# W2 of three feed-forward groups in four as seven products with the tokens down the partitions, summed in DRAM

## Chip, cores and metric

The kernel runs on one core of a Trainium2 chip. The metric is the time of one launch in microseconds of device time; the median of several runs stands for a kernel. The engines are TensorE (PE in the profile, with PEld for its weight loads), VectorE (DVE), ScalarE (ACT), GpSimd (POOL) and SyncE (SP), which here only issues DMAs.

## The reference, cut to what matters

Two layers, each with three token mixers on one input projection and then a feed-forward part; SEQ is 512, D_MODEL 1024, D_FF 4096, all in float32:

```
u = rms_norm(x)
[A | B | C | gates] = u @ w_in
x = x + (sigmoid gates * (branch A, B, C, projected)) @ w_out
x = x + relu(rms_norm(x) @ W1)^2 @ W2
```

The change is in the last line. W1 is 1024 by 4096, W2 4096 by 1024.

## The kernel before

**Products.** Activations lie transposed: features down the partitions, the 512 tokens along the columns. A float32 product goes in three passes over two parts of each operand, called hi and lo (type float32r): hi by hi, hi by lo, lo by hi. Weights come from DRAM in quarters of [128, 1024] floats (512 KB). SP loads a quarter into `stage`, ACT casts it to `w_hi`, DVE subtracts to give `w_lo` (`cut_to`, in the tags `hi` and `lo` of the pool `p_w`, six buffers each).

**The feed-forward part** (`mlp`). It starts with eight units `wo` (the end of the attention half), the sum of squares `ms`, and the row factors `rb`. Then come four groups. A group makes 1024 of the 4096 hidden features by W1, as four pairs of units. A pair is done as seven products of a Winograd form instead of eight (`pair`, `cut_pair`): each product has 12 matmuls of 256 columns, so a pair has 84, in PSUM tiles that the trace calls `x` (x17, x26, x45). ACT squares the relu of the outputs `c`, and ACT and DVE split them into `mh` and `ml`. The group's eight units of W2 follow, each 8 k-tiles times 3 passes = 24 matmuls of 512 columns (PSUM tile `w2`, in the trace `w`); weights are the stationary operand, `mh` and `ml` move. The first group's unit outputs are copied to `mo`, those of the next two are added to `mo` by DVE, after the third `mo` is scaled by the token factor `rs` and added to `h`, and the fourth group's are scaled into `y` and added to `h`; `ready` hands each finished row block to the next layer, whose first projection is `rv`.

**Order.** `mlp_order` weaves the next group's first two pairs of W1 into the W2 of the group before, after units 3 and 6 (`WOVEN`). All instructions are first noted, then `Plan.order` simulates a run of the engines with a price for each instruction (`price`, and `LATENCY` and `HOPS` between engines), and each engine takes the first of its ready instructions by key. So the order of every engine's stream follows from prices, from buffer counts (`BUFS_W`, `BUFS_STAGE`), and from how far ahead weights are called for (`prefetch`, `AHEAD_LOAD`, `AHEAD_SPLIT`). At run time each engine executes its stream strictly in that order. Before the change POOL issues no DMA and does nothing in the feed-forward part.

In the trace every matmul has line L411, every transpose L413, and all other engine work L417, since one helper issues them; names of tiles tell groups apart.

Of the kernel before, what the change touches and what calls it, by code (L numbers as in the profile page):

```python
# [17 lines left out]
L = 2  # L18
# [10 lines left out]
# positions of the small per-layer vectors in the row that every partition receives  # L29
# [20 lines left out]


def mlp_order():
    """W1 goes by pairs of units, W2 by units, in four groups of eight; a group's W1 starts within the W2 before it."""
    pairs = lambda g, k: [("w1", g, 2 * i) for i in k if g < 4]
    seq = pairs(0, range(4))
    for g in range(4):
        n = 0
# [9 lines left out]
def weight_plan():  # L67
    """Quarters of [128, 1024] in the order in which the core uses them: (key, matrix, rows, columns)."""
# [40 lines left out]
    for what, g, i in mlp_order():  # L109
# [3 lines left out]
        else:  # L113
            a_unit(("w2", g, i), "w_mlp_out", cols(i * 128, 128), r0=g * 1024)
    return plan
# [5 lines left out]
# units whose weights are used two by two, in seven products instead of eight (Winograd's form of Strassen's)  # L121
PAIRED = {WIDX["w1", f] for f in range(0, 32, 2)} | {WIDX["gate", n, i] for n in GATE_PAIRS for i in range(GATE_PAIRS[n], 8, 2)}

BUFS_STAGE = 2
BUFS_W = 6
BUFS_WH = 2
BUFS_MID = 3
AHEAD_LOAD = 6
AHEAD_SPLIT = 2
# [27 lines left out]

class Ref:
    """A view of such a tile."""
# [82 lines left out]
class Op:  # L242
    __slots__ = ("engine", "name", "args", "kwargs", "key", "cost", "deps", "tiles", "new", "left", "outs", "end",
                 "ready")
# [1302 lines left out]
```

## Time and profile before

| | |
|---|---|
| median of 3 runs | 1793.13 us (1792.23 to 1793.45) |
| span of the profiled execution | 1791.8 us |
| instructions | 26264 |
| granted TensorE clock | 1.00 in every slice |
| PE, DVE, ACT, POOL busy, shares of the span | 99%, 77%, 55%, 17% |

The launch has six stretches that can be told apart by the matmuls: an attention half and a feed-forward part per layer, with the eight `wo` units between them. The table of stretches further down gives each engine's busy time in one. Busy time of one instruction is longer than its share of a stream where instructions overlap in the pipeline, so the cost of one more instruction is read from the distance between the starts of neighbours (its pitch), not from its duration.

### The profile page before, as it was taken

The numbers are of one execution on the slowest core, as the hardware profiler recorded it, in microseconds if no ns is written. First come the engines' busy times: TensorE is split into PE (matmuls) and PEld (weight loads), VectorE is DVE, ScalarE is ACT, GpSimd is POOL, SyncE is SP. The second block draws the span as 40 slices with busy tenths as digits, with TensorE's granted clock in tenths as the row PEclk, the third lists the DMA queues.
The fourth block names the chain that finished last, engine by engine and source line by source line (L and its number), as shares of the span: only waits on it lengthen the run. The fifth ranks groups of instructions, "written<-read, shape, count | busy, mean of one in ns | idle before, by whom it ended". The sixth has DMA issues, their size and how long they took to land.

```text
span 1791.8 us, 26264 instructions
## 1 busy us (share of the span) xinstructions
PE 1767.7 (99%) x10216; PEld 1544.8 (86%) x10216; DVE 1376.4 (77%) x2084; ACT 983.2 (55%) x1568; POOL 297.1 (17%) x294
## 2 busy tenths in 40 slices
PE   8999999999999999999999999999999999999999
PEld 6887888889989989999888778888888899989897
DVE  7866797899979766678656677968999797566783
ACT  5545666784446655445444455768844466444450
POOL 3334472002210000000013335700111100000000
PEclk9999999999999999999999999999999999999999
DMA  6311212112352323333432121121133423234331
GB/s 203 105 61 49 93 49 79 59 37 95 107 170 101 118 94 118 123 115 116 152 106 71 48 80 62 59 63 56 39 104 130 159 83 134 95 102 128 121 113 56
DMA packets 53691, 172.50 MB, mean 96 GB/s; under 512 B 6336, under 2 KB 6848, under 8 KB 53568
## 3 DMA queue, kind: packets, MB, share of 16 engines
q1 hardware_dynamic: 53568, 170.84, 29.4%
q8 instruction: 80, 1.31, 0.3%
q14 instruction: 43, 0.35, 0.1%
HBM read 162.43 MB, written 8.39 MB: 95 GB/s over the span
## 4 chain that ended last, share of the span: by engine, by line
PE 82%; DVE 8%; issue 3%; POOL 3%; ACT 2%; DMA 1%; SPq 0%; DVEq 0%; ACTq 0%; POOLq 0%
PE x L411 21%; PE w L411 20%; PE gate L411 6%; PE proj L411 5%; PE wo L411 5%; PE c L411 4%; PE wtr L413 2%; PE rv L411 2%; DVE w_lo L417 2%; PE rg L411 2%; PE rq L411 2%; PE dsc L411 2%; PE gav L411 2%; PE gsc L411 2%; DVE c L417 1%
## 5 line engine op out<-in xcount | busy, mean ns | idle before, releaser
L417 ACT CAST w_hi<-stage 128x1024 fp32r<-128x1024 f32 (+1 forms) x283 | 276.6, 982 | 319.7 <-PE w L411 120.7
L417 DVE TENSOR_TENSOR w_lo<-stage,w_hi 128x1024 fp32r<-128x1024 f32 (+1 forms) x283 | 336.9, 1192 | 78.7 <-ACT w_hi L417 75.8
L411 PE MATMUL x<-u,w_hi 128*128 128x256 f32 x1472 | 273.5, 284 | 5.3 <-DVE c L417 5.3
L411 PEld LDWEIGHTS x<-u,w_hi 128*128 128x128 f32 x1472 | 232.3, 192 | 10.9 <-DVE c L417 8.2
L411 PE MATMUL x<-u,w_lo 128*128 128x256 f32 x736 | 208.0, 283 | 0.0
L411 PE MATMUL w<-ml,w_hi 128*128 128x512 f32 (+1 forms) x520 | 200.3, 386 | 0.0
L411 PE MATMUL w<-mh,w_lo 128*128 128x512 f32 (+1 forms) x520 | 200.1, 386 | 0.0
L411 PE MATMUL w<-mh,w_hi 128*128 128x512 f32 (+1 forms) x520 | 200.1, 387 | 0.0
L411 PEld LDWEIGHTS x<-u,w_lo 128*128 128x128 f32 x736 | 141.1, 192 | 0.0
L417 ACT ACTIVATE c<-c 128x512 f32<-128x512 f32 x156 | 98.4, 631 | 32.9 <-DVE c L417 30.2
L411 PEld LDWEIGHTS w<-mh,w_lo 128*128 128x128 f32 x520 | 97.8, 188 | 19.5
L411 PEld LDWEIGHTS w<-ml,w_hi 128*128 128x128 f32 x520 | 97.8, 188 | 18.7
L411 PEld LDWEIGHTS w<-mh,w_hi 128*128 128x128 f32 x520 | 97.8, 188 | 18.5
L411 PE MATMUL gate<-u,w_hi 128*128 128x512 f32 x320 | 107.3, 399 | 0.0
L411 PE MATMUL x<-t23h,w_lo 128*128 128x256 f32 x368 | 104.2, 283 | 0.0
L411 PE MATMUL x<-t23l,w_hi 128*128 128x256 f32 x368 | 104.0, 283 | 0.0
L411 PE MATMUL x<-t23h,w_hi 128*128 128x256 f32 x368 | 103.9, 283 | 0.0
L417 ACT CAST w_hi<-sa 128x1024 fp32r<-128x1024 f32 x46 | 48.5, 1053 | 77.0 <-DVE sa L417 55.9
L411 PE MATMUL c<-w_hi,u 128*128 128x512 f32 x256 | 86.1, 394 | 0.0
L417 POOL TENSOR_TENSOR gth<-gth,c 128x512 f32<-128x512 f32 x28 | 45.9, 1647 | 179.0 <-DVE c L417 179.0
L417 DVE TENSOR_TENSOR c<-x,pu 128x512 f32<-128x512 f32 x92 | 63.1, 686 | 12.0 <-PE x L411 11.3
L411 PEld LDWEIGHTS x<-t23l,w_hi 128*128 128x128 f32 x368 | 70.6, 192 | 0.0
(278 smaller groups left out, 4554.5 us busy)
## 6 DMA issues: line engine op xcount, KB each, us to landing
stage<-in_w SPq DMA_DIRECT2D x283, 512.0 KB, 3.6
h<-in_x SPq DMA_DIRECT2D x16, 256.0 KB, 5.3
mid<-h SPq DMA_DIRECT2D x16, 256.0 KB, 2.0
h<-mid SPq DMA_DIRECT2D x16, 256.0 KB, 4.8
keep<-h SPq DMA_DIRECT2D x8, 256.0 KB, 4.1
h<-keep SPq DMA_DIRECT2D x8, 256.0 KB, 3.9
out<-h SPq DMA_DIRECT2D x7, 256.0 KB, 2.0
t_ret<-in_t_ret SPq DMA_DIRECT2D x4, 256.0 KB, 4.9
```

Of the source, the lines that this page charges most:

```text
L411: self.nc.tensor.matmul(k.pop("out"), **k)
L413: self.nc.tensor.transpose(k["out"], k["in_"], k["identity"])
L417: getattr(getattr(self.nc, o.engine), o.name)(**k)
```

## The change

Groups 0, 1 and 2 of each layer (`WIDE_GROUPS`) do W2 in another form; group 3 keeps the eight plain units.

In a wide group the outputs have tokens down the partitions: the activations are the stationary operand (128 by 128) and W2 moves, 512 columns at a time. With W2 of the group as 2 by 2 blocks and the activations as 2 by 2 blocks, seven products are made (`WIDE_PRODUCTS`, left operands `WIDE`), each in two halves k and for two token tiles s: 24 matmuls of 512 columns per product. W1's outputs `c` are kept unsplit, and `rights` makes the right operands `xh`, `xl` from them.

The operands of the products come in three ways. A11, A12 and A22 (`cut_dma`): a DMA of POOL writes the quarter, cast, to `w_hi`; ACT writes its negative to `w_lo`; a second DMA of POOL adds the quarter onto `w_lo`. S1: a load by SP into a buffer `sa` and a DMA of POOL that adds the second quarter. S2, S4 and S3: DVE adds staged quarters; all four S are split by ACT and DVE as before.

Each product's two PSUM banks are copied by ACT to `wp` and go to `sums` in DRAM: in group 0 by plain DMAs of SP, in groups 1 and 2 by accumulating DMAs of POOL. In group 3, `gather` reads the 14 sums back, combines them with DVE, transposes the result on TensorE (PSUM tile `turn`), scales it and adds it to `h`. Its two halves stand at units 0 and 3 of that group.

Besides, `WOVEN` is (2, 4) in wide groups, `BUFS_W` falls from 6 to 5, the tag `sa` has three buffers, the prefetch goes by steps instead of quarters, the planner's price of a float32r matmul rises from 2.5 to 13.7 ns plus columns, and POOL's DMAs get prices. These alter the order of the attention half too. The diff also drops comments and docstrings; those lines are left out below.

```
-WOVEN = (3, 6)
...
+GATHERED = (0, 3)
...
+WIDE_GROUPS = (0, 1, 2)
...
+WOVEN = {True: (2, 4), False: (3, 6)}
...
-        for i in range(8):
-            while n < len(WOVEN) and WOVEN[n] == i:
+        n, wide = 0, g in WIDE_GROUPS
+        for i in range(7 if wide else 8):
+            while n < 2 and WOVEN[wide][n] == i:
...
+WIDE = ("A11", "A12", "A22", "S1", "S2", "S4", "S3")
+WIDE_PRODUCTS = (1, 2, 4, 5, 6, 3, 7)
...
-BUFS_W = 6
+BUFS_W = 5
...
-AHEAD_LOAD = 6
-AHEAD_SPLIT = 2
+AHEAD = 2
...
         if k["rhs"].tile.dtype == F32R:
-            return 2.5 + n / 2.4 * (1 if n >= 256 else 4)
+            return 13.7 + n / 2.4 * (1 if n >= 256 else 4)
...
+        o.late = self.LATENCY.get(engine, 0.0)
+        if engine == "gpsimd" and name == "dma_start":
+            o.cost, o.late = (880.0, 5600.0) if "accum_op" in kwargs else (600.0, 3800.0)
...
-        self.p_s = pool("s", 1)
+        self.p_s = pool("s", {"sa": 3, "sb": 1})
...
+    def cut_dma(self, q):
+        nc = self.nc
+        hi, lo = self.parts(self.p_w, 1024)
+        nc.gpsimd.dma_start(out=hi, in_=self.a["w"][q])
+        nc.scalar.activation(out=lo, in_=hi, func=AF.Copy, scale=-1.0)
+        nc.gpsimd.dma_start(out=lo, in_=self.a["w"][q], accum_op=ALU.add)
+        return hi, lo
...
+    def cut_wide(self, q, op, k):
+        nc = self.nc
+        at = lambda x: q + (int(x[1]) - 1) * 4 + (int(x[2]) - 1) * 2 + k
+        w = self.wide
+        def add(t, x):
+            nc.vector.tensor_tensor(out=t, in0=t, in1=self.load(at(x)), op=ALU.add)
+        if op == "A11":
+            w[k] = self.load(at("A21"), self.p_s, "sa")
+            nc.gpsimd.dma_start(out=w[k], in_=self.a["w"][at("A22")], accum_op=ALU.add)
+        if op[0] == "A":
+            return self.cut_dma(at(op))
+        if op == "S3":
+            w[k] = self.load(at("A21"))
+        if op != "S1":
+            add(w[k], {"S2": "A11", "S3": "A11", "S4": "A12"}[op])
+        return self.part(self.p_w, 1024, w[k])
+
+    def weights(self, l, key, k=0):
+        i = l * NS + STEP_AT[key] + k
+        self.prefetch(i + 1 + AHEAD)
+        return self.w[i]
...
+                    if g in WIDE_GROUPS:
+                        m.append(c)
+                        continue
...
+            if g in WIDE_GROUPS:
+                if i == 0:
+                    rights = self.rights(m)
+                    nxt = next(rights)
+                now, nxt = nxt, next(rights, None)
+                self.wide_product(l, g, i, now)
+                continue
+            if i == 0:
+                gather = self.gather(h, mid, load, r2)
+            if i in GATHERED:
+                next(gather)
...
-            if g == 0:
-                total[i] = self.g("mo")
-                nc.scalar.copy(out=total[i], in_=p)
-            elif g < 3:
-                nc.vector.tensor_tensor(out=total[i], in0=total[i], in1=p, op=ALU.add)
-                if g == 2:
-                    nc.vector.tensor_tensor(out=total[i], in0=total[i], in1=r2, op=ALU.mult)
-                    nc.vector.tensor_tensor(out=h[i], in0=h[i], in1=total[i], op=ALU.add)
...
+    def rights(self, m):
...
+        sub = lambda out, x, y: nc.vector.tensor_tensor(out=out, in0=x, in1=y, op=ALU.subtract)
+        t1 = []
+        for n in WIDE_PRODUCTS:
+            if n == 4:
+                for j in range(4):
+                    b1, b2 = m[j], m[4 + j]
+                    if j % 2 == 0:
+                        t1.append(self.g("t1"))
+                    sub(b1[:, rt], b2[:, rt], b1[:, rt])
+                    nc.vector.tensor_tensor(out=b1[:, lt], in0=b1[:, rt], in1=b1[:, lt], op=ALU.add)
+                    sub(b2[:, lt], b2[:, lt], b1[:, lt])
+                    sub(t1[-1][:, j % 2 * 256:j % 2 * 256 + 256], b2[:, rt], b1[:, lt])
+            out = []
+            for i in range(2):
+                hi, lo = self.g("xh", F32R), self.g("xl", F32R)
...
+                        self.split(x, hi[:, c], lo[:, c])
...
+    def wide_product(self, l, g, o, x):
...
+        ps = [self.psum("mm", f"wide{n}") for _ in range(2)]
+        for k in range(2):
+            hi, lo = self.weights(l, ("w2", g, o), k)
+            xh, xl = x[k]
+            for s in range(2):
+                for j in range(2):
+                    t = slice(j * 256 + s * 128, j * 256 + s * 128 + 128)
+                    c = slice(j * 512, j * 512 + 512)
+                    self.passes(ps[s], [(xh[:, t], hi[:, c]), (xh[:, t], lo[:, c]), (xl[:, t], hi[:, c])],
+                                k == 0 and j == 0, k == 1 and j == 1)
+        for s, p in enumerate(ps):
+            y = self.g("wp")
+            nc.scalar.copy(out=y, in_=p)
+            if g == WIDE_GROUPS[0]:
+                nc.sync.dma_start(out=self.sums[n, s], in_=y)
             else:
+                nc.gpsimd.dma_start(out=self.sums[n, s], in_=y, accum_op=ALU.add)
+
+    def gather(self, h, mid, load, r2):
+        def back(n, s):
+            x = self.g("wp")
+            nc.sync.dma_start(out=x, in_=self.sums[n, s])
+            return x
...
+        for s in range(2):
+            p1, p2, p6, p5, p3 = (back(n, s) for n in (1, 2, 6, 5, 3))
+            tt(p2, p1, p2)
+            tt(p6, p6, p1, ALU.subtract)
+            tt(p5, p5, p6)
+            tt(p3, p3, p5, ALU.subtract)
...
+        for half in range(2):
+            if half:
+                for s in range(2):
+                    p7, p4 = back(7, s), back(4, s)
+                    p6, p5 = u2[s]
+                    tt(p5, p5, p7, ALU.subtract)
+                    tt(p6, p6, p7, ALU.subtract)
+                    tt(p6, p6, p4)
...
+            for i in range(4):
+                k = half * 4 + i
+                h[k] = load(mid, k)
+                p = self.psum("tr", "turn")
+                for t in range(4):
+                    self.transpose(p[:, t * 128:(t + 1) * 128], c[half][t][:, i * 128:(i + 1) * 128])
                 y = self.g("y")
                 nc.vector.tensor_tensor(out=y, in0=p, in1=r2, op=ALU.mult)
...
+                nc.vector.tensor_tensor(out=h[k], in0=h[k], in1=y, op=ALU.add)
+            yield
```

Three places in the order of the engines. The first is POOL at the end of the first layer's attention half, where `gth` is a sum of gated branches and `vmu` belongs to the next layer's projection `rv`. Before:

```order
L417 TENSOR_TENSOR gth_3656<-gth_3656,c1_5396 128x512
L417 TENSOR_TENSOR gth_3882<-gth_3882,c0_5507 128x512
L417 TENSOR_TENSOR gth_4001<-gth_4001,c1_5568 128x512
L417 TENSOR_SCALAR vmu_9338<-vsum_9330 128x4
L417 TENSOR_TENSOR rs_9347<-ms_9341,mhalf_109 128x4
```

After, from the same sum on:

```order
L466 TENSOR_TENSOR gth_4017<-gth_4017,c1_5577 128x512
L466 DMA sa_6043<-in_w 128x1024
L466 DMA sa_6178<-in_w 128x1024
L466 DMA w_hi_6355<-in_w 128x1024
L466 DMA w_hi_6395<-in_w 128x1024
L466 DMA w_lo_6417<-in_w 128x1024
L466 DMA w_hi_6451<-in_w 128x1024
L466 DMA w_lo_6463<-in_w 128x1024
L466 DMA w_hi_6500<-in_w 128x1024
L466 DMA w_lo_6524<-in_w 128x1024
L466 DMA w_lo_6573<-in_w 128x1024
L466 DMA w_hi_6657<-in_w 128x1024
```

The feed-forward part now puts operand and sum DMAs into POOL's stream, one behind the other, where there was nothing between the two layers.

The second place is PE in the first group of layer 0. Before, a unit of W2 has the weight `w_hi` or `w_lo` stationary (named behind the comma) and `mh` or `ml` moving:

```order
L411 MATMUL w2_6498<-mh_6523,w_hi_6366 128x512
L411 MATMUL w2_6498<-ml_6537,w_hi_6366 128x512
L411 MATMUL w2_6498<-mh_6523,w_lo_6382 128x512
L411 MATMUL w2_6553<-mh_6169,w_hi_6386 128x512
L411 MATMUL w2_6553<-ml_6192,w_hi_6386 128x512
L411 MATMUL w2_6553<-mh_6169,w_lo_6405 128x512
```

After, around the start of product 4, whose operand A22 is `w_hi_6657` and `w_lo_6722`:

```order
L460 MATMUL x45_6752<-t4h_6066,w_hi_6489 128x256
L460 MATMUL x45_6752<-t4l_6075,w_hi_6489 128x256
L460 MATMUL x45_6752<-t4h_6066,w_lo_6511 128x256
L460 MATMUL wide4_6810<-w_lo_6722,xh_6482 128x512
L460 MATMUL wide4_6810<-w_hi_6657,xl_6502 128x512
L460 MATMUL wide4_6810<-w_hi_6657,xh_6482 128x512
L460 MATMUL wide4_6810<-w_lo_6722,xh_6482 128x512
L460 MATMUL wide4_6810<-w_hi_6657,xl_6502 128x512
L460 MATMUL wide4_6812<-w_lo_6722,xh_6482 128x512
```

The weight parts have become the moving operand, the activation parts `xh` and `xl` the stationary one, and the part that two DMAs of POOL and one copy of ACT write is read right behind the pairs of W1.

The third place is PE where W2 of the last group of layer 0 starts. Before:

```order
L411 MATMUL x26_8819<-u07_6000,w_lo_8711 128x256
L411 MATMUL w2_8930<-mh_8391,w_hi_8733 128x512
L411 MATMUL w2_8930<-ml_8404,w_hi_8733 128x512
L411 MATMUL w2_8930<-mh_8391,w_lo_8753 128x512
L411 MATMUL w2_8930<-mh_8407,w_hi_8733 128x512
```

After, `wp` being the combined sums that were read back:

```order
L460 MATMUL w2_9279<-mh_8679,w_lo_9216 128x512
L462 MATMUL turn_9338<-ident_235,wp_8937 128x128
L462 MATMUL turn_9338<-ident_235,wp_8989 128x128
L462 MATMUL turn_9338<-ident_235,wp_9070 128x128
L462 MATMUL turn_9338<-ident_235,wp_9080 128x128
L460 MATMUL w2_9279<-mh_8894,w_hi_9199 128x512
L460 MATMUL w2_9279<-ml_8905,w_hi_9199 128x512
L460 MATMUL w2_9279<-mh_8894,w_lo_9216 128x512
```

Transposes of the gathered sums, four to a tile, stand between the matmuls of the last group's units.

## Rows read from the trace of the kernel before

**Rows 1.** Page, section 1: busy time, share of the span, instructions.

```profile
span 1791.8 us, 26264 instructions
PE 1767.7 (99%) x10216; PEld 1544.8 (86%) x10216; DVE 1376.4 (77%) x2084; ACT 983.2 (55%) x1568; POOL 297.1 (17%) x294
```

**Rows 2.** Busy time by stretch: attention and feed-forward of layer 0, then of layer 1.

```profile
core 0: us, PE busy (x) PEld busy (x) DVE busy (x) ACT busy (x) POOL busy (x), PEclk, DMA share, GB/s
0.00:517.60 517.60, 504.32 (x2781) 430.24 (x2782) 425.68 (x678) 309.99 (x536) 153.95 (x156) 1.00 0.28 91
...
561.20:898.30 337.10, 337.10 (x2125) 306.73 (x2125) 242.41 (x335) 171.93 (x237) 0.00 (x0) 1.00 0.37 118
898.30:1406.00 507.70, 500.77 (x2777) 427.38 (x2776) 406.07 (x640) 294.67 (x509) 137.93 (x136) 1.00 0.25 78
...
1450.00:1791.80 341.80, 337.96 (x2151) 308.24 (x2149) 228.25 (x319) 157.09 (x216) 0.00 (x0) 1.00 0.32 105
```

**Rows 3.** Chain of waits through layer 0 feed-forward: start, us, what, matmuls.

```profile
by line: PE w L411 49.9%; PE x L411 46.1%; PE wo L411 1.8%; PE rv L411 1.7%; PE ms L411 0.4%; PE rb L413 0.1%
...
569.99 0.44 PE rb L413 x4
...
630.41 15.21 PE w L411 x67
645.62 8.63 PE x L411 x72
...
856.08 42.19 PE w L411 x186
898.26 6.12 PE rv L411 x27
```

**Rows 4.** Timeline of PE: start, us, instruction.

```profile
390.77 0.82 PE L413 MATMUL wtr<-ident,gE 128*128 128x128 f32 x6
391.34 0.48 PE L411 MATMUL gate<-u,w_hi 128*128 128x512 f32 x1
```

**Rows 5.** Timeline of DVE where its instructions stand back to back.

```profile
685.50 0.68 DVE L417 TENSOR_TENSOR sb<-stage,sa 128x512 f32<-128x512 f32 x1
686.10 0.41 DVE L417 TENSOR_TENSOR c<-x,c 128x256 f32<-128x256 f32 x1
686.44 0.68 DVE L417 TENSOR_TENSOR w_lo<-stage,w_hi 128x512 fp32r<-128x512 f32 x1
687.04 1.22 DVE L417 TENSOR_TENSOR w_lo<-sa,w_hi 128x1024 fp32r<-128x1024 f32 x1
688.19 0.69 DVE L417 TENSOR_TENSOR c<-x,pu 128x512 f32<-128x512 f32 x1
```

**Rows 6.** Groups of instructions by shape, layer 0 feed-forward: busy, mean ns | idle before.

```profile
L417 ACT CAST w_hi<-stage 128x1024 fp32r<-128x1024 f32 x52 | 54.7, 1051 | 96.2 <-PE w L411 61.3 <-PE x L411 20.4 <-DMA stage<-in_w 11.8
L417 DVE TENSOR_TENSOR w_lo<-sb,w_hi 128x1024 fp32r<-128x1024 f32 x15 | 18.3, 1219 | 5.2 <-ACT w_hi L417 5.2
L417 DVE TENSOR_TENSOR mo<-mo,w 128x512 f32<-128x512 f32 x16 | 11.0, 687 | 27.8 <-PE w L411 27.8
L417 ACT COPY mo<-w 128x512 f32<-128x512 f32 x8 | 4.6, 579 | 0.0
```

**Rows 7.** DMA in a quiet part of the feed-forward part, 600 to 850 us.

```profile
DMA packets 8369, 28.49 MB, mean 114 GB/s; under 512 B 928, under 2 KB 928, under 8 KB 8352
...
stage<-in_w SPq DMA_DIRECT2D x49, 512.0 KB, 3.6
h<-mid SPq DMA_DIRECT2D x8, 256.0 KB, 4.8
```

**Rows 8.** DMA where it is fullest, 5 to 12 us.

```profile
DMA packets 1150, 2.62 MB, mean 375 GB/s; under 512 B 125, under 2 KB 125, under 8 KB 1150
...
stage<-in_w SPq DMA_DIRECT2D x1, 512.0 KB, 6.8
```

**Rows 9.** Tile mTl, DVE beside POOL: ns min/median/max.

```profile
L417 DVE SCALAR_TENSOR_TENSOR mTl<-gth,mTh x16: 677/1235/1790, 471.8 to 1411.0; 128x512 fp32r<-128x512 f32 x16
```

**Rows 10.** Page, section 5: POOL's sums of gated branches: busy, mean ns.

```profile
L417 POOL TENSOR_TENSOR gth<-gth,c 128x512 f32<-128x512 f32 x28 | 45.9, 1647 | 179.0 <-DVE c L417 179.0
```

More of the change, by code (lines that the diff above doesn't have):

```diff
@@ L112, in weight_plan @@
                 a_unit(("w1", f), "w_mlp_in", cols(f * 128, 128))
-        else:
+        elif g not in WIDE_GROUPS:
             a_unit(("w2", g, i), "w_mlp_out", cols(i * 128, 128), r0=g * 1024)
+        elif i == 0:
+            for c in range(2):
+                for j in range(2):
+                    for k in range(2):
+                        r = g * 1024 + j * 512 + k * 256
+                        plan.append((("w2", g, c + 1, j + 1, k), "w_mlp_out", np.arange(r, r + 256), cols(c * 512, 512)))
     return plan
@@ L122, with steps @@
 PAIRED = {WIDX["w1", f] for f in range(0, 32, 2)} | {WIDX["gate", n, i] for n in GATE_PAIRS for i in range(GATE_PAIRS[n], 8, 2)}
+WIDE = ("A11", "A12", "A22", "S1", "S2", "S4", "S3")
+WIDE_PRODUCTS = (1, 2, 4, 5, 6, 3, 7)
+def steps():
+    out, at = [], {}
+    q = 0
+    while PLAN[q][0][0] != "w1":
+        at[PLAN[q][0]] = len(out)
+        out.append(("pair" if q in PAIRED else "one", q))
+        q += 2 if q in PAIRED else 1
+    for what, g, i in mlp_order():
+        at[(what, g * 8 + i) if what == "w1" else (what, g, i)] = len(out)
+        if what == "w1":
+            out.append(("pair", WIDX["w1", g * 8 + i]))
+        elif g in WIDE_GROUPS:
+            out += [("wide", WIDX["w2", g, 1, 1, 0], WIDE[i], k) for k in range(2)]
+        else:
+            out.append(("one", WIDX["w2", g, i]))
+    return out, at
+STEPS, STEP_AT = steps()
+NS = len(STEPS)
 BUFS_STAGE = 2
-BUFS_W = 6
+BUFS_W = 5
 BUFS_WH = 2
 BUFS_MID = 3
-AHEAD_LOAD = 6
-AHEAD_SPLIT = 2
+AHEAD = 2
 BUFS_G = 51
@@ L155, in tile, with __init__ @@
         return Tile(self, shape, dtype, tag or name, name).ref()
+class Pools:
+    def __init__(self, each):
+        self.each = each
+    def tile(self, shape, dtype, tag=None, name=None):
+        return self.each[tag].tile(shape, dtype, tag=tag, name=name)
 class Ref:
@@ L242 @@
 class Op:
-    __slots__ = ("engine", "name", "args", "kwargs", "key", "cost", "deps", "tiles", "new", "left", "outs", "end",
-                 "ready")
+    __slots__ = ("engine", "name", "args", "kwargs", "key", "cost", "late", "deps", "tiles", "new", "left", "outs",
+                 "end", "ready")
 class Plan:
@@ L397, in order @@
                 result.append(pick)
-                heapq.heappush(events, (now + o.cost + self.LATENCY.get(e, 0.0), 0, pick))
+                heapq.heappush(events, (now + o.cost + o.late, 0, pick))
                 heapq.heappush(events, (busy[e], 2, pick))
@@ L458, in __init__ @@
         nc.sync.dma_start(out=self.gains, in_=a["gains"])
-        self.loaded = self.cut = 0
-        self.stage, self.w = {}, {}
+        self.cut = 0
+        self.w, self.wide = {}, {}
     def tables(self):
@@ new lines, in mlp @@
+            nc.vector.tensor_tensor(out=y, in0=p, in1=r2, op=ALU.mult)
+            nc.vector.tensor_tensor(out=h[i], in0=h[i], in1=y, op=ALU.add)
+            ready(i, h[i])
+    def rights(self, m):
+        nc = self.nc
+        lt, rt = slice(0, 256), slice(256, 512)
+        sub = lambda out, x, y: nc.vector.tensor_tensor(out=out, in0=x, in1=y, op=ALU.subtract)
[13 more added lines that the diff above has]
+                hi, lo = self.g("xh", F32R), self.g("xl", F32R)
+                if n == 5:
+                    self.split(t1[i], hi, lo)
+                else:
+                    for j in range(2):
+                        k = 2 * i + j
+                        x = m[k if n in (1, 6, 7) else 4 + k][:, lt if n in (1, 2, 4, 6) else rt]
+                        c = slice(j * 256, j * 256 + 256)
+                        self.split(x, hi[:, c], lo[:, c])
+                out.append((hi, lo))
+            yield out
@@ L1435, in trunk @@
             tiles.append(k.ref())
+    core.sums = {}
+    for n in WIDE_PRODUCTS:
+        for s in range(2):
+            k = Tile(None, [128, 512], F32, None, "sums")
+            k.real = p_dram.tile([128, 512], F32, name=f"sums{n}{s}")
+            core.sums[n, s] = k.ref()
     def load(src, i):
```

97 lines of the change are left out of this document (40 added, 57 removed).

## The prediction

> **What bounds the kernel now.** First the page: TensorE (PE) is busy in 99% of the span, DVE in 77%, ACT in 55%, POOL in 17% [rows 1]. That is an average, so the table of stretches comes next. In a layer's feed-forward part PE is busy in all of the 337.1 us of layer 0, DVE in 242.4, POOL not at all, and DMA moves 118 GB/s; only in the attention halves is PE idle, 13.3 and 6.9 us [rows 2]. The chain of waits through layer 0's feed-forward part says the same in another way: it never leaves PE, half of it in W2 (`w`) and nearly half in W1 (`x`), and PE goes from the last `w` at 856.08 + 42.19 = 898.27 us straight into the next layer's `rv` [rows 3]. So here the end is set by the sum of matmul pitches, and a matmul less is worth its pitch as long as nothing else becomes late. Pitches: 512 columns 15.21 / 67 = 0.227 us, 256 columns 8.63 / 72 = 0.120 [rows 3].
>
> As a test of these prices: a layer has 32 units of 24 matmuls and 16 pairs of 84, 768 x 0.227 + 1344 x 0.120 = 335.6 of the 337.1 us.
>
> **Matmuls removed and added.** A wide group has 7 x 24 = 168 matmuls of 512 columns instead of 8 x 24 = 192. Over six wide groups that is 144 less: -144 x 0.227 = -32.7 us. A matmul with the weights moving is taken at the same price, since shape and passes are the same. Added are 64 transposes of 128 by 128. Six of them stood in (391.34 - 390.77) = 0.57 us, 0.095 each [rows 4]; the four of `rb` took 0.44, 0.11 each [rows 3]. So 6.1 to 7.0 us; I take 6.5. Net on PE -26.2 us, all on the path that sets the end. One wide group with its four pairs is now 336 x 0.120 + 168 x 0.227 = 78.5 us of PE, before 83.9.
>
> **DVE.** Its pitch, from starts of neighbours back to back, is 0.60 us for 512 elements, 0.34 for 256, 1.15 for 1024 [rows 5]. A pair costs five of 512 and three of 1024 for its weights, two of 512 and three of 256 for its outputs: 8.7 us, 34.7 for four. Before, a group added eight splits of `c`, eight `w_lo` and eight `mo`: 53.5 of 83.9 us, 64%. A wide group adds 8 `w_lo` and 6 sums of 1024, 24 splits and 16 subtractions of 256, and 2 splits of 512: 16.1 + 13.6 + 1.2 = 30.9, together 65.6 of 78.5 us, 84%. It is still under PE, so I count it at nothing; the cover is 12.9 us in a group. ACT has more cover: its idle time before the casts alone is 96 us in a layer [rows 6].
>
> **Does POOL take that cover?** POOL issues some 23 DMAs in a wide group, where it did nothing. The one place where the trace has POOL and DVE at work together is the end of the attention half: `mTl` takes 0.68 us alone but 1.24 in the median [rows 9], beside POOL's adds of 1.65 us [rows 10]. If each DMA issue held a DVE instruction up by the same 0.56 us, a group would lose 23 x 0.56 = 12.9 us of DVE, just the cover. Below that it costs nothing. The bounds for the time are 0 and about +18 (rival 2); I take 0.
> The Trainium skill, "SBUF — State Buffer", section "Who interferes with whom", says that a DVE instruction with two inputs in SBUF contends with a GpSimd instruction that reads SBUF, not with one that only writes it. The row of `mTl` agrees for adds, which read; issuing a DMA would only write descriptors, and by that rule the 12.9 us would be nothing. No row of before shows it.
>
> **The operand chain, the added wait.** For A11, A12 and A22 the path is: a slot of `p_w` comes free when its last matmul has run, POOL's DMA writes `w_hi`, ACT writes `w_lo`, POOL's second DMA adds onto it, PE reads it. Before it was shorter: the stage was loaded well ahead, and only ACT's cast waited for the slot (61.3 us of its idle time are for a `w` matmul [rows 6]). ACT's copy is 1.05 us [rows 6]. A 512 KB DMA takes 3.6 us to land when DMA is quiet [rows 7] and 6.8 when it is full [rows 8]. So the chain is 3.6 + 1.05 + 3.6 = 8.3 us at least. At most it is 6.8 + 1.05 + 6.8 and, if adding means that the target is read too, 0.524 MB / 375 GB/s = 1.4 more, 16.0 us. What does it have? In the order of PE, between the last reader of the slot of `w_hi_6657` and the first reader of `w_lo_6722` there are 19 matmuls of 512 and 84 of 256: 14.4 us. Counted so, the A operands of all wide groups have 12.9 to 14.6 us, apart from the first one of a group. So they are between 6 early and 3.1 us late. Operands come late together, in two clusters per group (A11 with A12, and A22), twelve over six groups: 0 to +37 us. POOL's queue carries the wait: behind a `w_lo` that waits for ACT stand the next `w_hi` and, in groups 1 and 2, the sums.
> Which end? Data of a wide group: 8 loads for pairs, 24 for W2's operands, 14 sums of 0.26 MB, 20.4 MB in 78.5 us, 260 GB/s. That lies 0.56 of the way from 114 [rows 7] to 375 [rows 8], so a DMA is put at 5.4 us and the chain at 11.9, a microsecond before it is due. I take three of the twelve clusters late by 1 us: +3.
> The Trainium skill, "Collectives: The Full Stack", section "The bandwidth ceiling: the fold count and why AG ≠ RS ≠ AR", says that an add made by the DMA needs two source reads. By it 7.9 MB more would be moved in groups 1 and 2, 361 GB/s, close to the fullest stretch [rows 8], the chain would be near its upper end, and the time that of rival 1; no run of before shows an adding DMA.
>
> **Gather and boundary.** The last sum that its first half needs is product 3 of group 2. From there ACT's copy 0.6 [rows 6], the adding DMA 3.6 to 6.8, the read back at 4.8 [rows 7] and eight DVE adds of 0.60, all pessimistically in a row, are 14 to 17 us. By the order PE has 22.7 us of other matmuls before the first transpose. The transposes stand in PE's stream, so if they are late PE stops. After the last pair of W1, counted in the order at these pitches, DVE now has 46 us of work in layer 0 beside 47 us of PE; before the change 30 beside 45. Bounds 0 and +5 for each layer; I take +2 in all.
>
> **Attention half.** The planner's new matmul price and five buffers for six reorder it. Rows of its effect don't exist; the bounds are the PE idle time that there is, 20 us over both layers, as a gain or as a loss [rows 2]. I take 0, with 7 either way as usual size, for the work itself is the same.
>
> **Sum.** 1791.8 - 26.2 + 3 + 2 = 1770.6 us of span; the median of before stands 1.3 us above the profiled span, so 1771.9, said as 1772.
>
> **Rivals.**
> 1. The operand chain is late, and the kernel ends no faster or slower. For it: 16.0 us at the upper end, POOL's single queue, 360 GB/s if adds read twice. Against: DMA was quiet before, and 11.9 us by the interpolated landing. At 12 clusters it eats the gain when it is late by (26.2 - 2) / 12 = 2.0 us, and is slower by over 0.2% from 2.3 us on. Late by 1 to 3.1 us it gives 1781 to 1806; at 2.3, 1797.
> 2. DVE becomes the bound in the wide groups, by POOL's interference on top of 84%. For it: [rows 9]. Then the waits of DVE for ACT, which cost nothing today, count as well: with 2 to 3 us in each of six groups 12 to 18 us, and the late boundary 5 more. It gives 1780 to 1795.
> 3. The attention half moves by its new order more than the feed-forward part: 1752 to 1792.
> That the columns don't go is excluded, since the order has 144 matmuls of 512 less.
>
> **How the numbers follow.** Measurement tells 0.2% (3.6 us) from no change. The forecast, 1764 to 1780, has 0.42, all of it faster. Rival 1 has 0.30: faster 0.06, same 0.06, slower 0.18. Rival 2 has 0.15: 0.08, 0.03, 0.04. Rival 3 has 0.13: 0.08, 0.02, 0.03. Sums: faster 0.64, same 0.11, slower 0.25. The range 1763 to 1804 leaves out the tail of rival 1 and both tails of rival 3.
>
> **What will show it.** In the profile after: `wide` at 0.227 us of pitch and a feed-forward part of 324 us in PE busy time confirm the first term. PE idle before `wide1`, `wide2` or `wide4` with a DMA of `w_lo` or `w_hi` as releaser is rival 1, and its landing times show which end of 8.3 to 16.0 holds. PE idle before `wide` for `xh`, `xl` or sums of DVE, and 512-element DVE work far above 0.69 us, is rival 2. PE idle before `turn` is the gather. The forecast is wrong if PE's idle time in the two feed-forward parts exceeds 10 us, or if the attention stretches change by more than 7.

## The result, and the profile after

The changed kernel takes 1872.86 us (median; 1870.22 to 1874.67) against 1793.06: 1.0446 times as long, 95% interval 1.0432 to 1.0461. The forecast was 1772, the range ended at 1804, and the sign was wrong. The profiled execution has a span of 1868.4 us.

The page of the changed kernel, section 1, to be held against [rows 1]:

```profile
span 1868.4 us, 27022 instructions
PE 1778.5 (95%) x10136; PEld 1533.3 (82%) x10136; DVE 1456.1 (78%) x2320; ACT 1073.9 (57%) x1780; POOL 409.5 (22%) x434
```

PE is busier than before although it has 144 matmuls of 512 columns less, and it is idle for 90 us. Where, the table of stretches tells (attention, feed-forward of layer 0, attention, feed-forward of layer 1; columns as in [rows 2] and to be held against it: us from start to end, length, busy time of PE, PEld, DVE, ACT and POOL, granted clock, DMA share, GB/s):

```profile
0.00:527.70 527.70, 508.04 (x2779) 429.14 (x2780) 417.49 (x677) 308.19 (x534) 153.99 (x156) 1.00 0.26 88
...
571.40:940.80 369.40, 338.59 (x2086) 302.10 (x2086) 287.99 (x456) 217.90 (x342) 56.27 (x70) 0.98 0.79 216
940.80:1457.40 516.60, 505.59 (x2782) 427.72 (x2781) 403.62 (x640) 293.75 (x510) 138.65 (x136) 1.00 0.23 77
...
1501.00:1868.40 367.40, 338.99 (x2108) 302.23 (x2106) 275.86 (x440) 203.91 (x323) 55.76 (x70) 0.98 0.76 207
```

The feed-forward parts are 32.3 and 25.6 us longer, where 13 less each was forecast; the attention halves are 10.1 and 8.9 longer, where nothing was forecast. Together 76.9 of the 76.6 us by which the span grew (the `wo` stretches differ by 0.3).

In the feed-forward parts the DMA share went from 0.37 to 0.79. The DMA view of 605 to 868 us, the wide groups of layer 0 (queue: packets, MB, share of 16 engines; then KB and median us to landing):

```profile
q0 software_dynamic: 9161, 26.78, 50.2%
q1 hardware_dynamic: 10031, 31.06, 34.5%
...
stage<-in_w SPq DMA_DIRECT2D x45, 512.0 KB, 5.2
w_lo<-in_w POOLq DMA_DIRECT2D x18, 512.0 KB, 7.4
w_hi<-in_w POOLq DMA_DIRECT2D x16, 512.0 KB, 6.5
```

q0 is POOL's queue, q1 SP's. POOL's moves less and its packets take longer. SP's own loads land in 5.2 us, before in 3.6 [rows 7]. From the first `wide` matmul of group 0 to that of group 1, and from there to that of group 2:

```profile
612.00:705.00 93.00, 82.79 (x507) 73.02 (x505) 63.40 (x97) 54.79 (x87) 10.51 (x14) 0.98 0.77 222
705.00:800.50 95.50, 83.88 (x506) 74.59 (x505) 67.15 (x109) 56.37 (x92) 22.73 (x28) 0.96 0.89 217
```

PE needs 78.5 us for either. The first, whose sums are not added, is nearly as long as the second, at a lower DMA share. What waits for what, over the whole run (us in total, times, longest):

```profile
PE x L460 <- DVE c L466: 25.8, 26, 2.5
PE wide L460 <- DMA w_lo<-in_w: 15.7, 13, 2.6
PE x L460 <- DVE w_lo L466: 11.0, 9, 3.1
...
ACT w_hi L466 <- DMA stage<-in_w: 132.3, 78, 6.7
```

Before, the last of these was

```profile
ACT w_hi L417 <- DMA stage<-in_w: 80.2, 62, 3.9
```

PE seldom waits for POOL's DMA itself (15.7 us). The larger wait is one step back: ACT's casts wait 132 us for SP's loads, before 80, DVE's sums of staged quarters 75 us, before 12, and PE follows DVE. The chain that ended last, between 560 and 690 us, leads not through PE as in [rows 3] but through those loads:

```profile
by line: DMA stage<-in_w 22.2%; DMA w_hi<-in_w 6.5%; DVE w_lo L466 5.7%; DVE c L466 4.9%; ACT w_hi L466 4.8%; issue 4.6%; DVE sa L466 3.6%; PE wide L460 3.4%; DVE xl L466 2.3%; PE x L460 2.1%; DVE sb L466 1.9%; DVE stage L466 1.9%; ACT c L4
```

And PE's granted clock, 1.00 in every slice before, falls in some slices in or behind which PE has stood (same columns as the table of stretches):

```profile
675.00:682.40 7.40, 6.92 (x42) 6.01 (x40) 3.36 (x5) 2.64 (x4) 0.57 (x1) 1.00 0.75 241
682.40:689.80 7.40, 5.37 (x30) 5.16 (x31) 5.27 (x7) 4.52 (x6) 0.00 (x0) 0.77 0.78 241
```

### The profile page after: what moved, and what is told of

Same layout as the page of the kernel before. It is cut to its first block, busy times and chain, and to the rows that moved or that the text cites. A ratio compares the mean times of both kernels' runs of the same rounds, so it can differ in the third digit from the quotient of the medians.

```text
span 1868.4 us, 27022 instructions
## 1 busy us (share of the span) xinstructions
PE 1778.5 (95%) x10136; PEld 1533.3 (82%) x10136; DVE 1456.1 (78%) x2320; ACT 1073.9 (57%) x1780; POOL 409.5 (22%) x434
## 3 DMA queue, kind: packets, MB, share of 16 engines
q0 software_dynamic: 20160, 58.73, 15.5%
## 4 chain that ended last, share of the span: by engine, by line
PE 26%; DMA 15%; DVE 13%; issue 6%; ACT 4%; POOL 4%; POOLq 0%; DVEq 0%; ACTq 0%; SPq 0%
DMA stage<-in_w 11%; PE w L460 5%; PE x L460 4%; DVE w_lo L466 4%; PE gate L460 3%; PE wo L460 2%; DMA w_lo<-in_w 2%; DVE sa L466 2%; PE proj L460 2%; PE wide L460 2%; ACT w_hi L466 2%; DVE c L466 1%; DVE sb L466 1%; DMA w_hi<-in_w 1%; PE rv L460 1%
## 5 line engine op out<-in xcount | busy, mean ns | idle before, releaser
L466 ACT CAST w_hi<-stage 128x1024 fp32r<-128x1024 f32 (+1 forms) x247 | 238.5, 970 | 262.4 <-DMA stage<-in_w 132.3
L466 DVE TENSOR_TENSOR w_lo<-stage,w_hi 128x1024 fp32r<-128x1024 f32 (+1 forms) x247 | 284.0, 1151 | 69.9 <-ACT w_hi L466 66.3
L460 PE MATMUL wide<-w_lo,xh 128*128 128x512 f32 x336 | 134.3, 400 | 15.8 <-DMA w_lo<-in_w 15.7
L460 PE MATMUL wide<-w_hi,xh 128*128 128x512 f32 x336 | 128.0, 395 | 4.4 <-ACT wp L466 3.0
L460 PE MATMUL wide<-w_hi,xl 128*128 128x512 f32 x336 | 131.8, 393 | 0.0
L466 DVE TENSOR_TENSOR w_lo<-sa,w_hi 128x1024 fp32r<-128x1024 f32 x82 | 100.0, 1219 | 17.4 <-ACT w_hi L466 17.4
L460 PEld LDWEIGHTS wide<-w_lo,xh 128*128 128x128 f32 x336 | 63.7, 190 | 33.4 <-DMA w_lo<-in_w 21.5
L466 POOL DMA_DIRECT2D sums<-wp x56 | 49.2, 897 | 154.8 <-ACT wp L466 108.1
L460 PEld LDWEIGHTS wide<-w_hi,xh 128*128 128x128 f32 x336 | 63.4, 190 | 19.2 <-ACT wp L466 5.3
L460 PEld LDWEIGHTS x<-t23h,w_lo 128*128 128x128 f32 x368 | 71.5, 195 | 8.1 <-DVE w_lo L466 8.1
```

The lines of the kernel that those rows point to most:

```text
L460: self.nc.tensor.matmul(k.pop("out"), **k)
L466: getattr(getattr(self.nc, o.engine), o.name)(**k)
```

## The experiments

### The attention halves: the planner's price

Edits to the kernel before (first run both lines, second the price alone):

```
-BUFS_W = 6
+BUFS_W = 5
...
-            return 2.5 + n / 2.4 * (1 if n >= 256 else 4)
+            return 13.7 + n / 2.4 * (1 if n >= 256 else 4)
```

Both together:

> The kernel before with two things of the change alone: the planner's price of a matmul (13.7 ns plus columns) and five weight buffers for six. Its attention halves then have nearly the order of the changed kernel's. If the new order of the attention halves is what made them 10.1 and 8.9 us longer, this run is 15 to 22 us slower than before (1808 to 1815) with both attention stretches longer and the feed-forward stretches within 3 us of 337 and 342. If the attention halves lose because the DMAs of the feed-forward part reach into them, it is within 4 us of before.

The price alone:

> The kernel before with the planner's new matmul price alone, six weight buffers kept. If the price is the cause of the longer attention halves, about +15 to +20 us; if the missing weight buffer is, within 4 us of before.

Measured: 1810.62 us (1.0103, interval 1.0088 to 1.0118) with both, 1809.28 (1.0095, 1.0078 to 1.0112) with the price alone. The attention halves of the run with the price alone, then layer 0's feed-forward part in the run with both:

```profile
0.00:525.50 525.50, 509.65 (x2781) 429.61 (x2782) 422.36 (x678) 310.31 (x536) 163.22 (x156) 1.00 0.28 90
...
906.50:1422.90 516.40, 507.17 (x2782) 428.45 (x2781) 405.71 (x640) 295.13 (x510) 150.31 (x136) 1.00 0.24 77
```

```profile
571.00:908.80 337.80, 337.67 (x2125) 306.72 (x2124) 243.89 (x338) 172.48 (x236) 0.00 (x0) 1.00 0.37 118
```

The attention halves become 7.9 and 8.7 us longer by the price, and the feed-forward part does not care. The missing buffer adds nothing to that. The reverse test puts the old price back, in the changed kernel, for the attention halves alone:

```
+MLP = [False]
...
-            return 13.7 + n / 2.4 * (1 if n >= 256 else 4)
+            return (13.7 if MLP[0] else 2.5) + n / 2.4 * (1 if n >= 256 else 4)
...
+        MLP[0] = True
         core.mlp(l, mT, h, mid, load, ready)
+        MLP[0] = False
```

> The changed kernel with the old price of a matmul (2.5 ns plus columns) in the attention halves and the new one in the feed-forward parts. If the new price alone lengthened the attention halves, they return to 518 and 508 us and the feed-forward parts stay at 369 and 367: 1853 to 1860 in all. If the five weight buffers or the new prefetch lengthen them as well, they stay above 522 and 512.

Measured: 1854.21 us, 1.0337 (1.0316 to 1.0357). The attention halves are back:

```profile
0.00:517.20 517.20, 504.16 (x2780) 429.51 (x2781) 419.17 (x677) 309.22 (x534) 156.71 (x156) 1.00 0.28 90
...
939.40:1448.80 509.40, 502.24 (x2781) 427.66 (x2780) 404.24 (x640) 294.31 (x509) 141.59 (x136) 1.00 0.25 78
```

The feed-forward parts took 378.5 and 372.3 us in this profiled execution, which is 12 us above the median of its runs; they did not gain. So some 17 us of the loss are the price, through the order that follows from it. 13.7 + 512 / 2.4 = 227 ns is just the pitch of [rows 3], and the order made with the truer price is the worse one. Which displaced instruction does it was not found. By the lines above and [rows 2], the price alone makes PE stand only 2.6 and 2.3 us longer; the other 5.3 and 6.4 us are longer busy time for the same matmuls, at the same granted clock of 1.00.

### The feed-forward parts: bytes, adds, buffers

Every adding DMA made plain, at the moment of issue, so that the order stays; what was to be added is left out:

```
             k = {a: v.resolve() if isinstance(v, Ref) else v for a, v in o.kwargs.items()}
+            k.pop("accum_op", None)
```

> The changed kernel in the same order, with every adding DMA of POOL made a plain write of the same bytes (so the sums, S1 and the lo parts lack what was to be added). Theory: the 16 DMA engines are the bound in the feed-forward part, since an adding DMA holds them about 1.7 times as long per byte (POOL's queue: 26.8 MB in 50% of 263 us, SP's 31.1 MB in 34.5%). Then POOL's queue falls to about 30%, the loads land sooner, and each feed-forward part loses 15 to 25 us: 1820 to 1840 in all. Rival: the chain of waits (slot, DMA, ACT, DMA, in POOL's one queue) is late by its hand-overs whatever the DMA engines carry: then it stays within 8 us of 1873.

Measured: 1823.90 us, 1.0171 (1.0143 to 1.0199), 49 less than the changed kernel. The page's queues, of the changed kernel and then of this run:

```profile
q1 hardware_dynamic: 63360, 191.82, 30.4%
q0 software_dynamic: 20160, 58.73, 15.5%
```

```profile
q1 hardware_dynamic: 63360, 191.82, 32.0%
q0 software_dynamic: 16576, 58.73, 9.8%
```

The same bytes. Here the packets of a MB of POOL's queue take, counted over all 16 engines, 0.098 x 1823.2 / 58.73 = 3.04 us, just as those of SP's. In the changed kernel 39.9 of the 58.7 MB are added (36 `w_lo` and 12 `sa` of 0.524, 56 sums of 0.262): 0.155 x 1868.4 - 18.9 x 3.04 = 232 us for 39.9 MB, 5.8 us a MB. An adding DMA takes 1.9 times as much of the engines' time as a plain one. The feed-forward parts:

```profile
570.70:913.30 342.60, 330.25 (x2085) 297.19 (x2084) 289.17 (x457) 217.01 (x342) 38.25 (x70) 1.00 0.69 233
...
1474.40:1823.20 348.80, 331.58 (x2109) 298.43 (x2107) 276.14 (x441) 204.31 (x323) 37.72 (x70) 0.99 0.66 218
```

26.8 and 18.6 us shorter: the rival, hand-overs that are late whatever the engines carry, is out as the main cause. About 20 us a part over the PE sum stay.

Next, A11, A12 and A22 loaded by SP like other weights:

```
-            return self.cut_dma(at(op))
+            return self.cut_one(at(op))
```

> The changed kernel with A11, A12 and A22 loaded by SP into the stage and split by ACT and DVE like all other weights, instead of by two DMAs of POOL. It takes 72 of POOL's DMAs away and 18 MB of SP loads come in their place; DVE gets 36 subtractions of 1024, 6.9 us in a group, 72.5 of 78.5. Theory (DMA engines the bound): feed-forward parts of 335 to 345 us, 1805 to 1830 in all. Rival (DVE, now at 92%, or two stage buffers are the bound): feed-forward parts stay above 355, 1845 or more.

Measured: 1879.41 us, 1.0495 (1.0472 to 1.0518), a little slower than the changed kernel: the theory of full DMA engines missed. Layer 0's feed-forward part:

```profile
571.30:949.00 377.70, 342.78 (x2085) 301.79 (x2084) 307.08 (x474) 216.78 (x342) 30.04 (x34) 0.98 0.65 186
```

DMA is less busy and the part is longer, so something else bounds it. A group now takes 22 loads through two stage buffers, where the changed kernel takes 16 (the two loads of `sa` have buffers of their own). The candidates were those buffers and DVE. In the changed kernel itself a third buffer (old price in the attention halves):

```
-BUFS_STAGE = 2
+BUFS_STAGE = 3
...
-BUFS_G = 51
+BUFS_G = 49
```

> As the run before, with three stage buffers instead of two (two buffers less in the pool of 51). Theory now: a wide group takes 18 loads through two stage buffers, one in 4.4 us, so a buffer has 8.7 us for landing (5.2), ACT's cast, DVE's subtraction and their queues; this cycle is what makes operands late. Then a third buffer takes 15 to 30 us from each feed-forward part (340 to 354) although the DMA engines carry the same bytes. Rival: the DMA engines themselves are full (79% busy), and a third buffer brings under 6 us a part, with landing times growing instead.

Measured: 1865.24 us, 1.0399 (1.0370 to 1.0428). The feed-forward parts:

```profile
566.00:928.80 362.80, 340.31 (x2086) 303.50 (x2085) 288.76 (x452) 216.65 (x342) 56.35 (x70) 0.97 0.82 218
...
1488.90:1867.70 378.80, 342.58 (x2109) 307.11 (x2107) 276.05 (x437) 202.82 (x323) 55.79 (x70) 0.96 0.74 198
```

That theory fell: against 378.5 and 372.3 of the run before, which has the same prices, one part is shorter, the other longer, and by the medians the run is 11 us slower (its attention halves, with the smaller pool, took 522.3 and 516.5). The growing landing times of the rival did not come either: from 610 to 850 us SP's loads landed in 5.3 us in both runs. With A loaded by SP, four buffers:

> A11, A12 and A22 loaded by SP into the stage and split by ACT and DVE, four stage buffers, old price in the attention halves. The DMA engines were busy only 65% of the feed-forward parts with two buffers, DVE 81%, and those parts took 378 and 376. If two buffers were the bound there: 335 to 345 each. If DVE is (by pitches 72.5 of 78.5 us in a group, plus its waits for ACT): 350 or more.

```
-BUFS_STAGE = 2
+BUFS_STAGE = 4
...
-BUFS_G = 51
+BUFS_G = 47
...
-            return self.cut_dma(at(op))
+            return self.cut_one(at(op))
```

Measured: 1810.51 us, 1.0103 (1.0069 to 1.0137). Layer 0's feed-forward part falls from 377.7 to 343.3, layer 1's from 376.1 to 348.1 (profiled executions 8 and 10 us above the medians of their runs):

```profile
569.60:912.90 343.30, 330.48 (x2085) 299.49 (x2085) 304.60 (x469) 218.24 (x343) 29.99 (x34) 0.98 0.71 203
```

So there the two buffers were the bound. An estimate from rows says the same: landing 4.7 us (that run, 605 to 850 us), cast 1.05 and subtraction 1.15 make 6.9 us a round, and 22 rounds through two buffers 76 us of a group's 78.5, while 16 rounds at a landing of 5.2 make 59. Loading A by SP helps only with more buffers. In the changed kernel, three buffers and plain writes:

> As the run with three stage buffers, and every adding DMA of POOL made a plain write of the same bytes (additions left out). With both causes gone, full DMA engines and two buffers, the feed-forward parts should come near the PE sum: 325 to 333 each, 1790 or less in all. If 340 or more remain, a third cause is at work: the chain of slot, DMA, ACT and DMA in POOL's queue, or DVE.

Measured: 1819.74 us, 1.0149 (1.0124 to 1.0173). The feed-forward parts:

```profile
566.70:912.20 345.50, 333.61 (x2085) 301.24 (x2084) 288.29 (x452) 215.97 (x342) 38.40 (x70) 0.98 0.69 229
...
1471.20:1814.60 343.40, 331.44 (x2109) 299.88 (x2107) 276.00 (x437) 202.00 (x323) 37.88 (x70) 0.99 0.67 218
```

Not the 325 to 333 expected, and no better than plain writes with two buffers (342.6 and 348.8). So no run shows that two stage buffers cost the changed kernel anything, and another cause is at work.

### Another cause: DVE in order behind sums that have not landed

The run with A loaded by SP and four buffers shows it. Stretches around the gather of layer 0, then DVE's timeline there (start, us, instruction, idle time before it and what ended it):

```profile
836.60:844.20 7.60, 5.96 (x50) 5.76 (x48) 1.86 (x3) 2.72 (x4) 0.89 (x1) 1.00 1.09 308
844.20:851.90 7.70, 1.65 (x7) 1.65 (x8) 5.39 (x8) 0.00 (x0) 0.00 (x0) 0.58 0.88 312
851.90:859.50 7.60, 7.60 (x51) 7.60 (x51) 6.70 (x11) 4.17 (x7) 0.00 (x0) 0.76 0.56 175
```

```profile
841.14 0.69 DVE L469 TENSOR_TENSOR wp<-wp 128x512 f32<-128x512 f32 x1 [5.50 <-DMA wp<-sums]
...
847.77 0.69 DVE L469 TENSOR_TENSOR wp<-wp 128x512 f32<-128x512 f32 x1 [2.31 <-DMA wp<-sums]
848.38 1.22 DVE L469 TENSOR_TENSOR w_lo<-sb,w_hi 128x1024 fp32r<-128x1024 f32 x1
849.51 0.68 DVE L469 TENSOR_TENSOR c<-x,pu 128x512 f32<-128x512 f32 x1
```

A sum is added, read back, and DVE's add for it stands in DVE's stream ahead of the `w_lo` and `c` that PE needs. DVE stands 5.5 and 2.3 us, PE 7.7 at once for such a `c`, and then PE runs at a lower clock. In the run just before, plain writes and three buffers, this cause is not alone: of PE's 11.9 idle us in layer 0, 6.0 are for DVE's `c` and 5.8 for ACT's copies to `wp`. First the buffers, paid for by a weight buffer instead of the pool of 51 (A loaded by SP):

```
-BUFS_STAGE = 2
-BUFS_W = 5
+BUFS_STAGE = 4
+BUFS_W = 4
```

> A11, A12 and A22 loaded by SP and split by ACT and DVE; four stage buffers paid for by a weight buffer (four instead of five) with the pool of 51 whole; old price in the attention halves; all else as in the changed kernel. If the attention halves of the run before with four stage buffers lost by the smaller pool, they return to 517 to 519 and 508 to 511 us. The feed-forward parts should stay at 343 to 350, since the gather still makes DVE wait for sums in its stream: about 1795 to 1803 in all.

Measured: 1811.02 us, 1.0101 (1.0086 to 1.0116). The attention halves return as expected, to 518.2 and 508.6; the feed-forward parts stay, at 346.3 and 346.8. The whole is above the 1795 to 1803 expected: these stretches add up to more than that. Then the order:

```
-GATHERED = (0, 3)
+GATHERED = (2, 5)
...
-WOVEN = {True: (2, 4), False: (3, 6)}
+WOVEN = {True: (3, 5), False: (3, 6)}
...
+        if engine == "sync" and MLP[0]:
+            o.late = 14000.0 if ins and ins[0].tile.name == "sums" else 6500.0
         if engine == "gpsimd" and name == "dma_start":
-            o.cost, o.late = (880.0, 5600.0) if "accum_op" in kwargs else (600.0, 3800.0)
+            o.cost, o.late = (880.0, 9000.0) if "accum_op" in kwargs else (600.0, 3800.0)
```

> As the run before it, and the planner told of longer landings in the feed-forward part (6.5 us for SP's loads, 14 for sums read back, 9 for adding DMAs), the gather at units 2 and 5 instead of 0 and 3, and the next group's pairs after products 3 and 5 instead of 2 and 4. Theory: what is left over the PE sum of 324 is DVE blocked in order behind sums that have not landed (and PE behind DVE); asked for later, they cost nothing: feed-forward parts of 326 to 334, 1772 to 1785 in all, faster than the kernel before. Rival: DVE at 92% is the bound and the parts stay at 340 or more, 1795 or slower.

Measured: 1770.21 us, 0.9872 (0.9858 to 0.9887), a little under the expected range. In this run and the next, units 0, 1 and 4 of the last group add their part to a row block that the gather loads only afterwards, so this part is left out of the result, though no instruction is. The stretches, and below them 80 us inside the wide groups:

```profile
561.80:886.20 324.40, 324.40 (x2085) 296.08 (x2084) 305.54 (x471) 217.06 (x343) 29.96 (x34) 1.00 0.74 214
...
1439.70:1768.30 328.60, 324.83 (x2109) 297.55 (x2107) 295.43 (x457) 204.72 (x324) 29.71 (x34) 1.00 0.69 200
```

```profile
600.00:680.00 80.00, 80.00 (x519) 73.31 (x518) 75.51 (x118) 55.37 (x91) 1.75 (x2) 1.00 0.73 223
```

PE is never idle in layer 0's part, and DVE, busy in 75.5 of 80 us, is still not the bound. The order alone took 21.9 and 18.2 us off. Three things were altered at once (told landing times, place of the gather, place of the pairs), so this run does not tell their shares. With this order and these buffers, the operands of A back by adding DMAs:

```
-            return self.cut_one(at(op))
+            return self.cut_dma(at(op))
```

> As the run before it in everything but one: A11, A12 and A22 again by two DMAs of POOL and a copy of ACT, as in the changed kernel. This prices that one step with buffers, order and gather out of the way. If adding DMAs fill the DMA engines: landing of their two DMAs above 6 us each, DMA busy above 75%, and feed-forward parts 20 to 45 us longer than in the run before, each. If the chain only lacked buffers and a better order: within 8 us of it.

Measured: 1836.71 us, 1.0246 (1.0229 to 1.0263). The feed-forward parts are 31.2 and 34.9 us longer than in the run before, and the landing times rise with them (layer 0, 600 to 860 us):

```profile
564.30:919.90 355.60, 336.58 (x2086) 302.88 (x2085) 288.01 (x453) 217.08 (x343) 56.20 (x70) 0.97 0.82 222
...
1472.00:1835.50 363.50, 337.35 (x2109) 304.09 (x2107) 277.52 (x439) 204.35 (x324) 55.73 (x70) 0.97 0.77 206
```

```profile
stage<-in_w SPq DMA_DIRECT2D x47, 512.0 KB, 5.4
w_lo<-in_w POOLq DMA_DIRECT2D x18, 512.0 KB, 6.2
w_hi<-in_w POOLq DMA_DIRECT2D x16, 512.0 KB, 5.8
```

This one step, priced with all else mended, is 66 us over both layers. `w_hi` landed in 5.8 us, a little under the expected 6. The step puts back the adds and the way through POOL's queue together: of PE's 19.0 idle us in layer 0, 8.8 are for A's DMAs and 9.6 for ACT's copies to `wp`; so this run does not tell the adds from the queue.

### A version that beats both

The run with the late gather, with the row blocks loaded by whichever of unit and gather comes first and handed on after both:

```
+                def row(k):
+                    if k not in rows:
+                        rows.add(k)
+                        h[k] = load(mid, k)
...
-            ready(i, h[i])
+            pend.append(i)
+            while pend and pend[0] < got:
+                k = pend.pop(0)
+                ready(k, h[k])
```

> The late-gather version with one thing mended: in the two runs before, units 0, 1 and 4 of the last group added their part to a row block before the gather had loaded it, so that part was lost. Now whichever of the two comes first loads the row block, and it is handed on when both have added. No instruction is added or removed. Theory: the same time as the run with the late gather, 1768 to 1774, faster than both the kernel before and the changed one; the feed-forward parts at 324 to 331. Rival: the loss of a dependency made that run fast, and the true one waits at the gather: 1780 or more.

Measured: 1769.52 us (1767.95 to 1770.28), 0.9875 times the kernel before (0.9858 to 0.9891). The same time without the part left out, as expected. Its page, feed-forward part of layer 0, and a piece of its chain of waits:

```profile
PE 1741.2 (99%) x10136; PEld 1523.5 (86%) x10136; DVE 1493.2 (84%) x2356; ACT 1073.3 (61%) x1780; POOL 359.0 (20%) x362
...
q1 hardware_dynamic: 68544, 210.69, 35.9%
q0 software_dynamic: 9792, 20.98, 7.2%
```

```profile
561.80:886.50 324.70, 324.44 (x2084) 295.90 (x2083) 305.01 (x471) 217.22 (x342) 30.00 (x34) 1.00 0.73 214
```

```profile
604.52 15.21 PE wide L465 x67
```

PE is at 99% again, and 67 `wide` matmuls take the 15.21 us that 67 of `w` took [rows 3]. In this kernel all that POOL's queue moves is added (12 `sa` and 56 sums): 0.072 x 1767.3 / 20.98 = 6.1 us a MB, against 0.359 x 1767.3 / 210.69 = 3.0 of SP's, so the price of an add is not one of A's alone.

## Why the prediction was wrong, by its own steps

**Matmuls: right.** Against [rows 2] the version that beats both saves 337.1 - 324.7 = 12.4 and 341.8 - 328.6 = 13.2 us, 25.6 together; the step said 26.2. The weights as moving operand cost the same 0.227 us, and eight `turn` took 0.79 us there, 0.10 each, as allowed. In the changed kernel itself the forecast's sign, 324 us of PE busy time in a feed-forward part, did not come: it was 338.6 and 339.0, by other steps.

**DVE and POOL: right.** The step that put POOL's 23 DMAs in a group at nothing holds. In the changed kernel, 605 to 868 us, DVE's instructions have the durations of [rows 5] and [rows 6], for one:

```profile
L466 DVE TENSOR_TENSOR w_lo<-sa,w_hi 128x1024 fp32r<-128x1024 f32 x28 | 34.2, 1221 | 8.1 <-ACT w_hi L466 8.1
```

Rival 2 is out in that form. The rule of the Trainium skill cited ahead ("SBUF — State Buffer", section "Who interferes with whom") agrees: `w_lo`, with `sa` and `w_hi` as inputs in SBUF, took 1221 ns beside POOL's DMAs, 1.22 us before.

**The operand chain: the step that failed.** It was put at 11.9 us, with 8.3 and 16.0 as ends, and priced at +3, at most +37. By the median landings it is 6.5 + 1.05 + 7.4 = 15 us; POOL's timeline, its DMAs paired in their order, has 8 us in the median from the issue of a `w_hi` to that of its `w_lo`, 17 at most, which with 7.4 comes to the same. That is at the far end, so rival 1 was the nearer case. But the choice of the end was not all: the upper bounds of all terms together (37, 18, 10 and 20) give 1793.1 - 26.2 + 85 = 1852, still 21 us too little. Two things in the step were wrong.
First the load. The step took 260 GB/s as 0.56 of the way to a full DMA, counting bytes, and left the second source read to a rival. By the measured 3.04 us a plain and 5.8 us an added MB, a group with adding sums has 18 loads of 0.524 MB by SP and six `w_hi`, 12.6 MB, and eight operands and 14 sums that are added, 7.9 MB: 38 + 46 = 84 us of all 16 engines in a group for which PE needs 78.5; group 0, with plain sums, has 74. The table of the two groups agrees: 0.89 x 95.5 = 85 and 0.77 x 93.0 = 72. Such a time is a sum over packets, not strictly what the engines can do, since a slice can show a share above 1 (1.09 in one of those above).
The Trainium skill ("Collectives: The Full Stack", section "The bandwidth ceiling: the fold count and why AG ≠ RS ≠ AR") states two source reads for the adds of a ReduceScatter. The 1.9 times measured here agree with it.
The run with plain writes alone shows what the adds cost the changed kernel: 26.8 + 18.6 = 45.4 us, with bytes, order and POOL's queue as they were; from 605 to 850 us `w_hi` and `w_lo` then landed in 4.9 and 5.0 us. Full engines are not the whole reason: 84 over 78.5 is 5.5 us in each of four groups, 22 in all, and group 0 lost 14.5 us with its 74 in 93.0. In the version that beats both the same two stretches take 78.5 and 79.0 us at shares of 0.72 and 0.85. How the rest divides between later landings, POOL's one queue and the order stays open.
Second the place. The step let only the 12 clusters of A be late. But SP's loads took 5.2 us to land instead of 3.6, and through them ACT, DVE and the pairs of W1 were late. PE's idle time in the two feed-forward parts is 30.8 + 28.4 = 59.2 us, where the prediction called itself wrong from 10 on. Of these 15.7 are for A's DMAs, and 35.0 are before `x`, for DVE's `c` and `w_lo` and ACT's `w_hi`, where none of its signs looked. Another 28 us are busy time of the same matmuls, 338.6 and 339.0 us against 324.4 and 324.8 in the run with the late gather, at a granted clock of 0.98; it had no term for that either. So the price of 37 us for rival 1 was too small as well: with its A operands back, the mended version loses 66.

**The attention halves: mis-sized.** The term was 0, with 7 usual and 20 as a bound from PE's idle time. It came out at +19.0, near the bound, and the planner's price alone gives 16.6. The sentence "the work itself is the same" was no reason for zero. Nothing in the rows told the sign, so the forecast's own range should have reached to both bounds. Nor is PE's idle time a bound for a loss: it limits what an order can gain, and of the 16.6 us only 4.9 are idle time, the rest longer busy time.

**The gather: right in the changed kernel, for the wrong reason.** There the loads were late before it. Where A came by SP through four buffers it became PE's largest stall, 7.7 us, since the sum that comes back takes an adding DMA and a read of 10 us in a full stretch (in the run with four buffers), not the 4.8 of a quiet one.

The size, 76.6 us of span, then is: 19.0 us of attention halves, and 45.0 and 38.8 by which the feed-forward parts exceed the 324.4 and 328.6 that the same matmuls take when fed, less the 25.9 gained. Of these 84, plain writes took 45 off in the changed kernel's own order; A's way by POOL, adds and queue together, costs 66 in the mended version, where order and buffers are other ones. The rest goes with the order around the gather and the pairs. These overlap, so no exact split is claimed.

## What to carry to other kernels

When a change moves work from a full engine to DMA, sum up the DMA engines' time as carefully as the matmuls, with an add at twice the price of a copy, compare it with the stretch that it has to fit, and ask which other loads share the engines. Buffers in front of a conversion bound the load rate to their number over the time of one round (landing, cast, subtraction; here 22 loads a group, 378 us with two buffers and 343 with four), so ask what more loads or a longer landing do to that round. An engine that works in order stands behind the first instruction whose data has not landed, so put such instructions late. A planner's prices are tuned together with its order: a truer price may give a worse order elsewhere, and it is worth confining it to the part for which it was measured.

## What the runs showed of the hardware

An adding DMA took 5.8 us (by difference) to 6.1 us (where all of the queue is added) of the 16 DMA engines' time a MB against 3.04 for a plain one, from SBUF to DRAM and from DRAM to SBUF taken together; plain DMAs of POOL, casting or not, taken together, took what those of SP did. PE's granted clock, at 1.00 throughout the kernel before, fell to 0.58, near the lower of its levels (1.2 of 2.4 GHz), in a slice in which PE was busy for 1.65 of 7.7 us and was still 0.76 in the next one, where PE was busy throughout. In the changed kernel, behind a wait of 3.1 us (876.1 to 879.3 us), matmuls of 256 columns started 0.21 us apart for 3.6 us, where 0.12 is their pitch [rows 3]; so a stall can cost more than its length.
